# The down projection of a decoder layer: seven block products for four feature chunks instead of eight

## The chip, the core and the metric

The kernel runs on one core of a Trainium2 chip. The core has five engines with a queue each, which run in program order and wait for one another by semaphores: TensorE (PE; its weight loads are listed as PEld), VectorE (DVE), ScalarE (ACT), GpSimd (POOL) and SyncE (SP), which issues the DMAs. The metric is the time of one execution on the device in microseconds: 2034.15 us before, the median of 3 runs (2033.97 to 2034.47).

## The reference

The kernel computes one decoder layer on x of 1024 tokens x 1024 features in float32: a half-weighted feed-forward pass, a token mixer (stick-breaking attention and a gated recurrence), a second half-weighted feed-forward pass, and a final norm. Cut to what the change touches:

```python
def swiglu(h, w_gate, w_up, w_down):
    return (jax.nn.silu(h @ w_gate) * (h @ w_up)) @ w_down
...
    for l in range(DEPTH):
        h = rmsnorm(x, ffn1_norm[l])
        x = x + 0.5 * swiglu(h, ffn1_w_gate[l], ffn1_w_up[l], ffn1_w_down[l])
...
        h = rmsnorm(x, ffn2_norm[l])
        x = x + 0.5 * swiglu(h, ffn2_w_gate[l], ffn2_w_up[l], ffn2_w_down[l])
```

w_gate and w_up are 1024 x 2816, w_down is 2816 x 1024.

## The kernel before

Everything is held transposed: features on the 128 partitions, tokens along the free axis. x is 16 tiles x[c, hf] of 128 features x 512 tokens: 8 feature chunks c, 2 token halves hf. The hidden dimension of a feed-forward pass is 22 chunks of 128, and the loop over f0 takes them in pairs.

**Split numbers.** A float32 operand is split into a rounded part H (ScalarE, L121) and a rest L (VectorE, or GpSimd where `eng` says so, L122). `mm3` (L124 to L127) then does H·H, H·L and L·H, three matmuls of 128x128 by 128x512, into one PSUM bank. A weight's parts are named uH and uL (pool `unit`, 4 buffers of each), an activation's aH and aL (4 of each), those of the normalised input hH, hL, bH, bL.

**Gate and up** of a pair of chunks (`gate_up`, L391) are a 2 x 2 block product: two chunks by two halves of the 1024 input features, times these halves by two token halves. `seven` (L362) forms it with seven block products in the way of Strassen and Winograd instead of eight. `combine` (L348) makes the seven weight blocks from the two loaded tiles (raw), with four additions on GpSimd in place (L352, L353, L354, L356) and seven splits; a block product is 4 x 3 = 12 matmuls, so gate and up of a pair are 2 x 84 = 168. The blocks of the input are made once per pass. The products' sums are taken on VectorE (L373) in float32 tiles of tag c; `up` multiplies by the gate (L399) and splits the result (`finish_act`).

**Down** of a pair (`down`, L406) is plain: for each of the 8 output chunks and each token half, the two chunks are accumulated in one bank, 6 matmuls, and VectorE adds half of it to x (L415). That is 2 x 8 x 6 = 96 matmuls a pair. Its weights are split with GpSimd's help.

The first pair of a pass (f0 = 0) is computed without blocks, and the last two pairs share one down with the sums for the norm that follows. PSUM banks are handed out in a fixed turn, seven of them (`bank`). The order of instructions on each engine is not that of the code: a scheduler arranges them by a timeline of its own, and the tile pools add the waits for free buffers.

Of the kernel before, what the change touches and what calls it, by code (L numbers as in the profile page):

```python
# [8 lines left out]
F32 = mybir.dt.float32  # L9
# [4 lines left out]
ALU = mybir.AluOpType  # L14

P = 128
# [11 lines left out]
def hybrid_layer(ctx: ExitStack, tc, xT, gains, wg1, wu1, wd1, w_in, lbl, w_out, wg2, wu2, wd2, outT):  # L28
# [222 lines left out]
    def ffn(wg, wu, wd, order, prepare, on_x, on_half, pieces, g0, shared):  # L251
        one, two = order
        with ExitStack() as st:
            raws = st.enter_context(tc.tile_pool(name="raw", bufs=3))
            unit = st.enter_context(tc.tile_pool(name="unit", bufs=4))
            hx = st.enter_context(tc.tile_pool(name="hx", bufs=12))
            ap = st.enter_context(tc.tile_pool(name="ap", bufs=7))
            acc = st.enter_context(tc.tile_pool(name="acc", bufs=5, space=bass.MemoryType.PSUM))
            turns = itertools.cycle(shared)

# [10 lines left out]
            def load(src):  # L271
                r = raws.tile([P, 2 * HALF], F32, tag="raw", name="raw")
                nc.sync.dma_start(r, src)
                return r

            def entry(src, pool=None, eng=None):

                p, tH, tL = (hx, "bH", "bL") if pool is hx else (unit, "uH", "uL")
                H = p.tile([P, HALF], F32R, tag=tH, name=tH)
                L = p.tile([P, HALF], F32R, tag=tL, name=tL)  # L280
                split(H, L, src, eng)
                return H, L

            def cols4(e, k):
                return [t[:, k % 4 * P:(k % 4 + 1) * P] for t in e]

            def finish_act(a, pool=None):
                if pool is hp:
                    H, L = [hp.tile([P, HALF], F32R, tag=t, name=t) for t in ("hH", "hL")]
                else:  # L290
                    H, L = [ap.tile([P, HALF], F32R, tag=t, name=t, bufs=4) for t in ("aH", "aL")]
                split(H, L, a)
                return H, L
# [51 lines left out]
                    block("4", k, b22, nc.vector)  # L345


            def combine(r0, r1):  # L348
                a11, a12, a21, a22 = r0[:, :HALF], r0[:, HALF:], r1[:, :HALF], r1[:, HALF:]
                tt = nc.gpsimd.tensor_tensor  # L350
                e = {"11": entry(a11), "12": entry(a12), "22": entry(a22)}
                tt(a22, a21, a22, op=ALU.add)  # L352
                tt(a21, a11, a21, op=ALU.subtract)  # L353
                tt(a11, a22, a11, op=ALU.subtract)  # L354
                e["s2"] = entry(a11)
                tt(a12, a12, a11, op=ALU.subtract)  # L356
                e["s3"] = entry(a21)
                e["s1"] = entry(a22)
                e["s4"] = entry(a12)
                return e  # L360

            def seven(r0, r1, done):  # L362

                e = combine(r0, r1)

                def product(a, b):
                    ps = bank()
                    for k in range(4):
                        mm3(ps, cols4(e[a], k), B[b, k], k == 0, k == 3)
                    return ps  # L370

                def add(out, a, ps):
                    nc.vector.tensor_tensor(out, a, ps, op=ALU.add)  # L373

                u2, c11, u3, c21 = [vec() for _ in range(4)]
                nc.scalar.copy(u2, product("11", "11"))
                add(c11, u2, product("12", "21"))
                done((0, one), c11)
                p4 = product("22", "4")
                add(u2, u2, product("s2", "2"))  # L380
                add(u3, u2, product("s3", "3"))
                add(c21, u3, p4)
                done((1, one), c21)
                p5 = product("s1", "1")
                add(u3, u3, p5)
                done((1, two), u3)
                add(u2, u2, p5)
                add(u2, u2, product("s4", "22"))
                done((0, two), u2)

            def gate_up(f0, pool=None):  # L391
                S, As = {}, {}

                def gate(key, t):
                    nc.scalar.activation(t, t, AF.Silu)
                    S[key] = t

                def up(key, t):
                    nc.vector.tensor_tensor(t, S[key], t, op=ALU.mult)  # L399
                    As[f0 % 4 + key[0], key[1]] = finish_act(t, pool)  # L400

                seven(load(wg[f0]), load(wg[f0 + 1]), gate)
                seven(load(wu[f0]), load(wu[f0 + 1]), up)
                return As

            def down(Ds, As, fs, hf, chunks, on_x=None, cols=slice(0, HALF), steps=None, at=()):  # L406

# [14 lines left out]
            for f0 in range(0, NF - 2, 2):  # L422
                last = f0 + 4 >= NF
                fs = [f0 % 4, f0 % 4 + 1]
                if f0 == 0:
# [8 lines left out]
                    for hf in order:  # L434
# [16 lines left out]
                        if hf == one:  # L451
                            blocks_one()
                    blocks_two()
                else:
                    if f0 == 4 and prepare is first_h:
                        lower_bound()
                    As = gate_up(f0)
                if last:
                    As.update(gate_up(f0 + 2, hp))
                    fs = fs + [(f + 2) % 4 for f in fs]  # L460
                Ds = {}
# [591 lines left out]
```

## Time and profile before

| | |
|---|---|
| median of 3 runs | 2034.15 us |
| the profiled execution's own time | 2031.69 us |
| its span, from the first to the last instruction | 2030.0 us |
| PE busy, of the span | 1974.2 us (97%) |
| DVE, ACT, POOL busy | 1326.2, 751.7, 559.3 us |
| DMA, mean busy share of 16 engines (q1) | 16.7% |
| mean granted TensorE clock | 0.989 |

The prediction is worked out from the profiled execution, which lies 2.5 us below the median of the runs. Matmuls are pipelined: each is listed with its whole duration, and the next starts before it ends. The two feed-forward passes reach from the start to about 680 us and from about 1330 us to the end; the mixer lies between them.

### The profile page before, as it was taken

How to read it: one execution, taken by the hardware profiler on the slowest of the kernel's cores; microseconds unless marked ns; L12 is line 12 of the kernel's file. 1: busy time of each engine (PE TensorE's matmuls, PEld its weight loads, DVE VectorE, ACT ScalarE, POOL GpSimd, SP SyncE). 2: the span in 40 equal slices, each digit the busy share in tenths (PEclk: the TensorE clock that was granted, in tenths of full speed). 3: DMA queues.
4: the chain of work that ended last, by engine and by line, in shares of the span. 5: the costliest groups of instructions: out<-in, count | busy, mean ns of one | idle time of the engine just before them, and what ended most of it. 6: DMA issues, size and time to landing. Idle time of an engine off the chain costs nothing.

```text
span 2030.0 us, 28718 instructions
## 1 busy us (share of the span) xinstructions
PE 1974.2 (97%) x11226; PEld 1645.4 (81%) x11226; DVE 1326.2 (65%) x2079; ACT 751.7 (37%) x1381; POOL 559.3 (28%) x569
## 2 busy tenths in 40 slices
PE   9799999999999999999999999999999999999998
PEld 7678888888888797887987977887788888888887
DVE  7975556566557647849659479578655665665574
ACT  6333222223324335535535345443232222233243
POOL 8533222222324301202102052006232223233243
PEclk9999999999999999999999999999999999999999
DMA  4022111111212211010010121210221121221112
GB/s 167 11 62 63 53 42 52 53 52 63 62 42 90 88 52 33 12 43 22 12 52 23 32 74 42 69 37 21 63 62 44 40 63 42 62 63 54 50 52 83
DMA packets 41255, 106.73 MB, mean 53 GB/s; under 512 B 4768, under 2 KB 6816, under 8 KB 41120
## 3 DMA queue, kind: packets, MB, share of 16 engines
q1 hardware_dynamic: 40832, 104.88, 16.7%
q8 instruction: 88, 1.44, 0.3%
q14 instruction: 47, 0.39, 0.1%
q10 hardware_dynamic: 288, 0.02, 0.0%
HBM read 96.49 MB, written 8.39 MB: 52 GB/s over the span
## 4 chain that ended last, share of the span: by engine, by line
PE 85%; DVE 11%; issue 2%; POOL 1%; ACT 1%; DMA 0%; SPq 0%; POOLq 0%; DVEq 0%; ACTq 0%
PE acc L127 20%; PE acc L125 20%; PE acc L126 20%; PE pj L125 3%; PE pj L126 3%; PE pj L127 3%; PE po L690 2%; PE pv L126 2%; PE pv L125 2%; DVE rest L651 2%; PE pv L127 1%; PE wo L125 1%; PE wo L126 1%; PE wo L127 1%; DVE hL L122 1%
## 5 line engine op out<-in xcount | busy, mean ns | idle before, releaser
L121 ACT CAST uH<-raw 128x512 fp32r<-128x512 f32 x424 | 256.4, 620 | 628.8 <-PE acc L126 473.7
L122 DVE TENSOR_TENSOR uL<-raw,uH 128x512 fp32r<-128x512 f32 x352 | 254.2, 737 | 142.0 <-ACT uH L121 134.5
L373 DVE TENSOR_TENSOR c<-c,acc 128x512 f32<-128x512 f32 x280 | 188.1, 683 | 223.0 <-PE acc L127 222.0
L415 DVE SCALAR_TENSOR_TENSOR x<-acc,x 128x512 f32<-128x512 f32 (+1 forms) x328 | 216.1, 674 | 122.0 <-PE acc L127 121.8
L125 PE MATMUL acc<-hH,uH 128*128 128x512 f32 x704 | 275.0, 392 | 7.1 <-ACT hH L121 3.7
L126 PE MATMUL acc<-hL,uH 128*128 128x512 f32 x704 | 276.3, 393 | 1.4 <-DVE hL L122 1.3
L127 PE MATMUL acc<-hH,uL 128*128 128x512 f32 x704 | 265.9, 391 | 2.8 <-DVE uL L122 2.8
L126 PE MATMUL acc<-aL,uH 128*128 128x512 f32 x576 | 221.8, 389 | 0.8 <-DVE aL L122 0.8
L127 PE MATMUL acc<-aH,uL 128*128 128x512 f32 x576 | 221.6, 389 | 0.0
L352 POOL TENSOR_TENSOR raw<-raw 128x512 f32<-128x512 f32 x40 | 52.3, 1308 | 589.5 <-issue 306.8
L125 PE MATMUL acc<-aH,uH 128*128 128x512 f32 x576 | 211.6, 389 | 0.0
L127 PE MATMUL acc<-bH,uL 128*128 128x512 f32 x480 | 186.5, 389 | 0.3 <-DVE uL L122 0.3
L125 PE MATMUL acc<-bH,uH 128*128 128x512 f32 x480 | 186.7, 389 | 0.0
L126 PE MATMUL acc<-bL,uH 128*128 128x512 f32 x480 | 186.7, 389 | 0.0
L125 PEld LDWEIGHTS acc<-hH,uH 128*128 128x128 f32 x704 | 133.0, 189 | 36.4 <-ACT hH L121 4.1
L127 PEld LDWEIGHTS acc<-hH,uL 128*128 128x128 f32 x704 | 132.8, 189 | 31.7 <-DVE uL L122 4.4
L126 PEld LDWEIGHTS acc<-hL,uH 128*128 128x128 f32 x704 | 133.1, 189 | 31.0 <-DVE hL L122 2.1
L122 POOL TENSOR_TENSOR uL<-raw,uH 128x512 fp32r<-128x512 f32 x72 | 96.3, 1339 | 175.6 <-ACT uH L121 173.6
L126 PEld LDWEIGHTS acc<-aL,uH 128*128 128x128 f32 x576 | 108.1, 188 | 23.6 <-DVE aL L122 1.2
L125 PEld LDWEIGHTS acc<-aH,uH 128*128 128x128 f32 x576 | 108.1, 188 | 22.5
L127 PEld LDWEIGHTS acc<-aH,uL 128*128 128x128 f32 x576 | 108.1, 188 | 22.4
L125 PE MATMUL pj<-hH,uH 128*128 128x512 f32 x304 | 121.1, 398 | 0.5 <-DVE q L587 0.5
(228 smaller groups left out, 3981.7 us busy)
## 6 DMA issues: line engine op xcount, KB each, us to landing
raw<-in_wd_dram SPq DMA_DIRECT2D x44, 512.0 KB, 3.7
raw<-in_wg_dram SPq DMA_DIRECT2D x40, 512.0 KB, 3.6
raw<-in_wu_dram SPq DMA_DIRECT2D x40, 512.0 KB, 3.6
raw<-in_w_in_dram SPq DMA_DIRECT2D x56, 256.0 KB, 2.6
x<-in_x_dram SPq DMA_DIRECT2D x16, 256.0 KB, 5.8
xs<-x SPq DMA_DIRECT2D x16, 256.0 KB, 2.0
raw<-in_w_out_dram SPq DMA_DIRECT2D x16, 256.0 KB, 2.7
x<-xs SPq DMA_DIRECT2D x16, 256.0 KB, 3.0
```

Source lines behind the costliest of these rows:

```text
L121: nc.scalar.copy(dH, src)
L122: (eng or nc.vector).tensor_tensor(dL, src, dH.bitcast(F32), op=ALU.subtract)
L125: nc.tensor.matmul(ps, lhsT=w[0], rhs=a[0], start=first, stop=False)
L126: nc.tensor.matmul(ps, lhsT=w[0], rhs=a[1], start=False, stop=False)
L127: pe(nc.tensor.matmul(ps, lhsT=w[1], rhs=a[0], start=False, stop=last))
L352: tt(a22, a21, a22, op=ALU.add)
L373: nc.vector.tensor_tensor(out, a, ps, op=ALU.add)
L415: done = nc.vector.scalar_tensor_tensor(xt, ps, 0.5, xt, op0=ALU.mult, op1=ALU.add)
L651: nc.vector.tensor_tensor_scan(rest[:, :n], rest[:, :n], rest[:, :n], 1.0 if diag else carry, ALU.mult, ALU.bypass)
L690: nc.tensor.matmul(po[:, (qp % 2) * 256:(qp % 2) * 256 + 256], lhsT=vs[b // 2][:, b % 2, a], rhs=w[:, 256 * i:256 * i + 256], start=m == q ...
```

## The change

Chunks 2 to 17 of each pass are now taken in four groups of four; chunks 0 and 1 and the last four stay as they were. `gate_up` of a pair hands over its four results unsplit; when the second pair of a group is done, `down_seven` projects all four chunks. For each pair it treats the product as 2 x 2 blocks (two halves of the 1024 output features, two token halves, two chunks) and forms seven products of blocks, called P1 to P7 here, in the order of the code. Each is four output chunks wide, and the two pairs (n = 0, n = 1) are accumulated in the same bank: 4 x 2 x 3 = 24 matmuls.

The weight blocks come from `combine`, which is now a generator, as the products ask for them; the splits of the first pair's are on VectorE, those of the second's on GpSimd. `act_blocks` makes the blocks of activations with four subtractions per pair on GpSimd. A product's banks are read once: P1's by ScalarE into a temporary u, that GpSimd adds to x (`onto`); P2, P3, P6 and P7 are added to x by VectorE; P4 and P5 are added to u by VectorE and from there to x by GpSimd. Four raw tiles are held instead of three, twelve temporaries instead of seven; `lower_bound`, a few small instructions for the mixer, moves by one round of the loop.

```diff
-            raws = st.enter_context(tc.tile_pool(name="raw", bufs=3))
+            raws = st.enter_context(tc.tile_pool(name="raw", bufs=4))
...
-            ap = st.enter_context(tc.tile_pool(name="ap", bufs=7))
+            ap = st.enter_context(tc.tile_pool(name="ap", bufs=12))
...
-            def combine(r0, r1):
-                a11, a12, a21, a22 = r0[:, :HALF], r0[:, HALF:], r1[:, :HALF], r1[:, HALF:]
+            def combine(a11, a12, a21, a22, eng=None):
+
                 tt = nc.gpsimd.tensor_tensor
-                e = {"11": entry(a11), "12": entry(a12), "22": entry(a22)}
+                yield entry(a11, eng=eng)
+                yield entry(a12, eng=eng)
+                yield entry(a22, eng=eng)
                 tt(a22, a21, a22, op=ALU.add)
                 tt(a21, a11, a21, op=ALU.subtract)
                 tt(a11, a22, a11, op=ALU.subtract)
-                e["s2"] = entry(a11)
+                yield entry(a11, eng=eng)
                 tt(a12, a12, a11, op=ALU.subtract)
...
+            def down_seven(f0, pairs):
+
+                es = []
+                for n in range(2):
+                    r0, r1 = load(wd[f0 + 2 * n]), load(wd[f0 + 2 * n + 1])
+                    es.append(combine(r0[:, :HALF], r1[:, :HALF], r0[:, HALF:], r1[:, HALF:],
+                                      nc.gpsimd if n else nc.vector))
+
+                def act_blocks(a):
+                    def less(o, p, q):
+                        nc.gpsimd.tensor_tensor(o, p, q, op=ALU.subtract)
+
+                    b11, b12, b21, b22 = a[0, one], a[0, two], a[1, one], a[1, two]
+                    yield finish_act(b11)
+                    yield finish_act(b21)
+                    less(b11, b12, b11)
+                    t = xp.tile([P, HALF], F32, tag="x", name="a2")
+                    less(t, b22, b11)
+                    less(b21, b21, t)
+                    less(b12, b22, b12)
+                    yield finish_act(b21)
+                    yield finish_act(t)
+                    yield finish_act(b12)
+                    yield finish_act(b11)
+                    yield finish_act(b22)
+
+                blocks = [act_blocks(a) for a in pairs]
+
+                def products():
+                    ws, bs = [next(e) for e in es], [next(b) for b in blocks]
+                    for c in range(4):
+                        ps = bank()
+                        for n in range(2):
+                            mm3(ps, cols4(ws[n], c), bs[n], n == 0, n == 1)
+                        yield c, ps
+
+                def half_onto(out, ps):
+                    nc.vector.scalar_tensor_tensor(out, ps, 0.5, out, op0=ALU.mult, op1=ALU.add)
+
+                def onto(c, hf, t):
+                    nc.gpsimd.tensor_tensor(x[c, hf], x[c, hf], t, op=ALU.add)
+
+                u = {}
+                for c, ps in products():
+                    u[c] = vec()
+                    nc.scalar.mul(u[c], ps, 0.5)
+                    onto(c, one, u[c])
+                for c, ps in products():
+                    half_onto(x[c, one], ps)
+                for c, ps in products():
+                    half_onto(x[c + 4, one], ps)
+                for c, ps in products():
+                    half_onto(u[c], ps)
+                    onto(c, two, u[c])
+                for c, ps in products():
+                    half_onto(u[c], ps)
+                    onto(c + 4, one, u[c])
+                    onto(c + 4, two, u[c])
+                for c, ps in products():
+                    half_onto(x[c, two], ps)
+                    half_onto(x[c + 4, two], ps)
+                for c, ps in products():
+                    half_onto(x[c, two], ps)
...
+                elif not last:
+                    if f0 == 6 and prepare is first_h:
+                        lower_bound()
+                    if f0 % 4 == 2:
+                        As = gate_up(f0, split_up=False)
+                    else:
+                        down_seven(f0 - 2, (As, gate_up(f0, split_up=False)))
+                    continue
                 else:
-                    if f0 == 4 and prepare is first_h:
-                        lower_bound()
                     As = gate_up(f0)
-                if last:
                     As.update(gate_up(f0 + 2, hp))
```

`seven` takes its blocks from the generator, and `gate_up` has a switch `split_up`, which leaves the split out.

**GpSimd's order at the start of the down projection.** Before, at a pair's end: the four splits of down weights, and behind them the additions for the next gate.

```order
L122 TENSOR_TENSOR uL_1713<-raw_1710,uH_1712 128x512 [waits DVE_49,DMAHW6_49,PE_49,Activation_49]
L122 TENSOR_TENSOR uL_1717<-raw_1710,uH_1716 128x512 [waits DVE_49,PE_49,Activation_49]
L122 TENSOR_TENSOR uL_1723<-raw_1720,uH_1722 128x512 [waits DVE_49,DMAHW7_49,PE_49,Activation_49]
L122 TENSOR_TENSOR uL_1727<-raw_1720,uH_1726 128x512 [waits DVE_49,PE_49,Activation_49]
L352 TENSOR_TENSOR raw_1860<-raw_1860 128x512 [waits DMAHW1_49,DVE_49,Pool_49]
L353 TENSOR_TENSOR raw_1860<-raw_1858,raw_1860 128x512 [waits DMAHW0_49,Pool_49]
L354 TENSOR_TENSOR raw_1858<-raw_1860,raw_1858 128x512 [waits Pool_49]
L356 TENSOR_TENSOR raw_1858<-raw_1858 128x512 [waits Pool_49]
```

Now, in the second group of the first pass, from the split of the second pair's weight for P2 (c is a float32 temporary, a_2618 the block t of the second pair, x_0 and x_1 are x of the first and second token half):

```order
L122 TENSOR_TENSOR uL<-raw,uH 128x512 [waits DVE_49,DMAHW3_49,PE_49,Activation_49]
L418 TENSOR_TENSOR c<-c 128x512 [waits DVE_49]
L448 TENSOR_TENSOR x_0_181<-x_0_181,c 128x512 [waits Activation_49]
L448 TENSOR_TENSOR x_0_201<-x_0_201,c 128x512 [waits Activation_49]
L418 TENSOR_TENSOR a_2618<-c 128x512 [waits Pool_49]
L418 TENSOR_TENSOR c<-c 128x512
L448 TENSOR_TENSOR x_0_222<-x_0_222,c 128x512 [waits Activation_49]
L354 TENSOR_TENSOR raw<-raw 128x512 [waits DMAHW1_49,DMAHW0_49,DVE_49]
L122 TENSOR_TENSOR uL<-raw,uH 128x512 [waits PE_49,Activation_49]
L448 TENSOR_TENSOR x_0_231<-x_0_231,c 128x512 [waits Activation_49]
L418 TENSOR_TENSOR c<-c,a_2618 128x512 [waits Pool_49]
L355 TENSOR_TENSOR raw<-raw 128x512 [waits Pool_49]
```

The subtractions for the activations, the additions of P1 onto x and the weight-block additions stand in one queue; the last of the four subtractions (c<-c,a_2618), which P3 needs, is the eleventh of these rows.

**GpSimd's order at the end of the down projection**, from the split of the second pair's weight for P7 to the additions of the next gate:

```order
L122 TENSOR_TENSOR uL<-raw,uH 128x512 [waits PE_49,Activation_49]
L448 TENSOR_TENSOR x_0_264<-x_0_264,c 128x512 [waits DVE_49]
L448 TENSOR_TENSOR x_1_350<-x_1_350,c 128x512
L448 TENSOR_TENSOR x_0_273<-x_0_273,c 128x512 [waits DVE_49]
L448 TENSOR_TENSOR x_1_359<-x_1_359,c 128x512
L448 TENSOR_TENSOR x_0_282<-x_0_282,c 128x512 [waits DVE_49]
L448 TENSOR_TENSOR x_1_368<-x_1_368,c 128x512
L448 TENSOR_TENSOR x_0_291<-x_0_291,c 128x512 [waits DVE_49]
L448 TENSOR_TENSOR x_1_377<-x_1_377,c 128x512
L354 TENSOR_TENSOR raw<-raw 128x512 [waits DMAHW5_49,DVE_49]
L355 TENSOR_TENSOR raw<-raw 128x512 [waits DMAHW4_49,Pool_49]
L356 TENSOR_TENSOR raw<-raw 128x512 [waits Pool_49]
```

The eight additions of P5 onto x stand ahead of the three (L354, L355, L356) from which the gate's block s2 is made; before, no addition onto x stood on GpSimd.

**VectorE's order in the down projection.** Before, in the down stage of a pair, the reads of PSUM waited for TensorE alone:

```order
L415 SCALAR_TENSOR_TENSOR x_0_181<-acc,x_0_181 128x512 [waits PE_49]
L415 SCALAR_TENSOR_TENSOR x_0_201<-acc,x_0_201 128x512 [waits PE_49]
L415 SCALAR_TENSOR_TENSOR x_0_222<-acc,x_0_222 128x512 [waits PE_49]
L415 SCALAR_TENSOR_TENSOR x_0_231<-acc,x_0_231 128x512 [waits PE_49]
L415 SCALAR_TENSOR_TENSOR x_1_315<-acc,x_1_315 128x512 [waits PE_49]
L415 SCALAR_TENSOR_TENSOR x_1_323<-acc,x_1_323 128x512 [waits PE_49]
L415 SCALAR_TENSOR_TENSOR x_1_332<-acc,x_1_332 128x512 [waits PE_49]
L122 TENSOR_TENSOR uL<-raw,uH 128x512 [waits DMAHW6_49,PE_49,Activation_49]
L415 SCALAR_TENSOR_TENSOR x_1_341<-acc,x_1_341 128x512 [waits PE_49]
```

Now, where P6 and P7 are read (x_1_315 and the next ones are chunks 0 to 3, x_1_350 and the next ones 4 to 7):

```order
L445 SCALAR_TENSOR_TENSOR x_1_315<-acc,x_1_315 128x512 [waits DVE_49,PE_49]
L445 SCALAR_TENSOR_TENSOR x_1_323<-acc,x_1_323 128x512 [waits DVE_49,PE_49]
L445 SCALAR_TENSOR_TENSOR x_1_350<-acc,x_1_350 128x512 [waits Pool_49]
L445 SCALAR_TENSOR_TENSOR x_1_332<-acc,x_1_332 128x512 [waits DVE_49,PE_49]
L445 SCALAR_TENSOR_TENSOR x_1_359<-acc,x_1_359 128x512 [waits Pool_49]
L122 TENSOR_TENSOR uL<-raw,uH 128x512 [waits DMAHW5_49,PE_49,Activation_49]
L445 SCALAR_TENSOR_TENSOR x_1_368<-acc,x_1_368 128x512 [waits Pool_49]
L445 SCALAR_TENSOR_TENSOR x_1_341<-acc,x_1_341 128x512 [waits DVE_49,PE_49]
L445 SCALAR_TENSOR_TENSOR x_1_377<-acc,x_1_377 128x512 [waits Pool_49]
```

Every second read of a bank of P6 now waits for GpSimd's addition onto the same tile, and the split of a weight for the next gate stands between them.

## Rows read from the trace of the kernel before

**Rows 1.** Page: the span, and busy time, share and instructions of each engine.
```profile
span 2030.0 us, 28718 instructions
...
PE 1974.2 (97%) x11226; PEld 1645.4 (81%) x11226; DVE 1326.2 (65%) x2079; ACT 751.7 (37%) x1381; POOL 559.3 (28%) x569
```

**Rows 2.** Chain of waits, 130 to 260 us: start, length, engine, tile, line.
```profile
136.47 0.91 PE acc L125 x4
...
196.08 0.68 PE acc L125 x3
...
255.92 0.68 PE acc L125 x3
```

**Rows 3.** Timeline of TensorE, 92 to 106 us: three matmuls that follow each other.
```profile
start us, us, engine line op out<-in xcount [idle before <-releaser]
...
93.17 0.39 PE L126 MATMUL acc<-hL,uH 128*128 128x512 f32 x1
93.40 0.39 PE L127 MATMUL acc<-hH,uL 128*128 128x512 f32 x1
93.62 0.39 PE L125 MATMUL acc<-hH,uH 128*128 128x512 f32 x1
```

**Rows 4.** Stage table, one pair of chunks: busy time (instructions) by engine, granted clock.
```profile
core 0: us, PE busy (x) PEld busy (x) DVE busy (x) ACT busy (x) POOL busy (x), PEclk, DMA share, GB/s
...
196.10:255.90 59.80, 59.80 (x265) 49.52 (x265) 35.68 (x53) 16.59 (x29) 15.52 (x12) 1.00 0.19 53
```

**Rows 5.** Timeline of GpSimd, 195.5 to 257 us, idle time before in brackets.
```profile
215.96 1.29 POOL L352 TENSOR_TENSOR raw<-raw 128x512 f32<-128x512 f32 x1 [20.50 <-issue]
217.32 1.29 POOL L353 TENSOR_TENSOR raw<-raw 128x512 f32<-128x512 f32 x1
218.69 1.29 POOL L354 TENSOR_TENSOR raw<-raw 128x512 f32<-128x512 f32 x1
220.06 1.30 POOL L356 TENSOR_TENSOR raw<-raw 128x512 f32<-128x512 f32 x1
...
246.27 1.29 POOL L122 TENSOR_TENSOR uL<-raw,uH 128x512 fp32r<-128x512 f32 x1 [7.19 <-ACT uH L121]
```

**Rows 6.** Timeline of GpSimd, 70 to 105 us.
```profile
95.75 1.71 POOL L330 TENSOR_TENSOR b<-b,b 128x512 f32<-128x512 f32 x1
97.43 1.72 POOL L354 TENSOR_TENSOR raw<-raw 128x512 f32<-128x512 f32 x1
99.10 1.73 POOL L330 TENSOR_TENSOR b<-b,b 128x512 f32<-128x512 f32 x1
100.79 1.74 POOL L356 TENSOR_TENSOR raw<-raw 128x512 f32<-128x512 f32 x1
102.48 1.74 POOL L330 TENSOR_TENSOR b<-b,b 128x512 f32<-128x512 f32 x1
```

**Rows 7.** Timeline of VectorE, 70 to 105 us.
```profile
91.05 0.68 DVE L122 TENSOR_TENSOR uL<-raw,uH 128x512 fp32r<-128x512 f32 x1
...
98.05 0.69 DVE L415 SCALAR_TENSOR_TENSOR x<-acc,x 128x512 f32<-128x512 f32 x1
98.65 1.04 DVE L122 TENSOR_TENSOR hL<-b,hH 128x512 fp32r<-128x512 f32 x1
99.73 1.66 DVE L311 SCALAR_TENSOR_TENSOR b<-x,gn,rstd 128x512 f32<-128x512 f32 x1
101.31 1.77 DVE L122 TENSOR_TENSOR uL<-raw,uH 128x512 fp32r<-128x512 f32 x1
```

**Rows 8.** Groups by line: count, busy us, mean ns, idle before and releasers.
```profile
L121 ACT CAST uH<-raw 128x512 fp32r<-128x512 f32 x424 | 256.4, 620 | 628.8 <-PE acc L126 473.7 <-PE pj L126 48.8 <-issue 47.3
L122 DVE TENSOR_TENSOR uL<-raw,uH 128x512 fp32r<-128x512 f32 x352 | 254.2, 737 | 142.0 <-ACT uH L121 134.5 <-PE acc L125 3.2 <-PE tp L126 1.8
...
L415 DVE SCALAR_TENSOR_TENSOR x<-acc,x 128x512 f32<-128x512 f32 (+1 forms) x328 | 216.1, 674 | 122.0 <-PE acc L127 121.8
...
L122 DVE TENSOR_TENSOR aL<-c,aH 128x512 fp32r<-128x512 f32 x80 | 74.5, 932 | 16.4 <-ACT aH L121 15.1
```

**Rows 9.** TensorE after waits, 50 to 57 and 92 to 106 us, and stage table.
```profile
55.90 1.12 PE L208 MATMUL pr<-ident,rs 128*128 128x128 f32 x4 [4.96 <-DVE rs L196]
...
98.17 0.51 PE L125 MATMUL acc<-hH,uH 128*128 128x512 f32 x1 [3.70 <-ACT hH L121]
...
101.19 0.63 PE L126 MATMUL acc<-hL,uH 128*128 128x512 f32 x1
101.62 0.63 PE L125 MATMUL acc<-hH,uH 128*128 128x512 f32 x1
...
100.00:101.00 1.00, 1.00 (x3) 0.81 (x4) 1.00 (x1) 0.84 (x2) 1.00 (x2) 0.50 0.00 0
...
103.00:104.00 1.00, 0.87 (x4) 0.74 (x5) 1.00 (x3) 0.00 (x0) 1.00 (x1) 1.00 0.00 0
```

More of the change, by code (lines that the diff above doesn't have):

```diff
@@ L354, in combine @@
                 tt(a11, a22, a11, op=ALU.subtract)
-                e["s2"] = entry(a11)
+                yield entry(a11, eng=eng)
                 tt(a12, a12, a11, op=ALU.subtract)
[L357 to L360, printed above, removed]
+                yield entry(a21, eng=eng)
+                yield entry(a22, eng=eng)
+                yield entry(a12, eng=eng)
             def seven(r0, r1, done):
-                e = combine(r0, r1)
+                e = dict(zip(("11", "12", "22", "s2", "s3", "s1", "s4"),
+                             combine(r0[:, :HALF], r0[:, HALF:], r1[:, :HALF], r1[:, HALF:])))
                 def product(a, b):
@@ L389, in seven, with gate_up @@
                 done((0, two), u2)
-            def gate_up(f0, pool=None):
+            def gate_up(f0, pool=None, split_up=True):
                 S, As = {}, {}
@@ L399, in up @@
                     nc.vector.tensor_tensor(t, S[key], t, op=ALU.mult)
-                    As[f0 % 4 + key[0], key[1]] = finish_act(t, pool)
+                    As[f0 % 4 + key[0] if split_up else key[0], key[1]] = finish_act(t, pool) if split_up else t
                 seven(load(wg[f0]), load(wg[f0 + 1]), gate)
```

## The prediction

> **What bounds the kernel now.** I read the page's table of engines first: TensorE is busy for 1974.2 of 2030.0 us [rows 1], GpSimd for 28% of the span. A busy matmul is no measure of its price, because matmuls overlap, so I went to the chain of waits next. In a feed-forward pass it is TensorE alone, and one mark comes back every 59.84 us: 136.47, 196.08, 255.92 [rows 2]. That is one pair of feature chunks: 2 x 7 x 12 = 168 matmuls for gate and up, 2 x 48 = 96 for down, 264 in all, so 0.2267 us each. The timeline of TensorE says the same: matmuls last 0.39 us and start 0.23 us apart [rows 3]. Between the marks nothing holds TensorE up. In the window of one pair [rows 4] VectorE is busy for 35.68 of 59.80 us, ScalarE for 16.59 and GpSimd for 15.52. These passes are bound by the number of matmuls, as long as the other three engines keep up inside each stage and not only on average.
>
> **What is removed.** Per four chunks the down projection goes from 2 x 96 = 192 matmuls to 7 x 4 x 6 = 168. That is 24 x 0.2267 = 5.44 us. There are four such groups in each pass, eight in all: 43.5 us. Had each matmul cost its 0.39 us, it would be 75; the start distance is the right price. DMA bytes do not change.
>
> **What is added, per group.**
> - ScalarE: 14 weight casts instead of 8, 14 activation casts instead of 8, and 4 copies out of PSUM: 16 x 0.62 = 9.9 us [rows 8]. It had 33 of 120 us busy, so TensorE covers this.
> - VectorE: 28 PSUM additions instead of 32, 14 splits of activations instead of 8, 7 weight splits that GpSimd did: -4 x 0.67 + 6 x 0.93 + 7 x 0.74 = 8.1 us [rows 8]. With 71 of 120 us before, this too fits on average.
> - GpSimd: 8 additions for the weight blocks, 8 for the activation blocks, 16 onto x, one split fewer: +31. It has 55 instructions per group instead of 24. At one per 1.37 us (the start distance of 215.96, 217.32, 218.69, 220.06; a split lasts the same 1.29 as an addition [rows 5]) this is 75 us in a group of 114. On average it fits; the stage decides.
>
> **The stage.** Take t = 0 at the first matmul of a group's first down product (P1), and the end at the fourth product of the next gate, whose weight block s2 needs three GpSimd additions that stand behind the last addition onto x (the listing of GpSimd's order at the end of the down projection). TensorE's work between the two is 168 + 36 = 204 matmuls, 46.2 us. GpSimd's is 6 weight splits, 8 weight-block additions, 4 for the activations of the second pair, 16 onto x and the 3 for the gate: 37 instructions in one queue.
>
> It cannot start earlier: the first of them splits the second weight of P2, whose buffer is freed by the last product of up, at t = 0, and needs a cast (0.62) first; call it 0.8. The next wants the last activation of up, ready at about 2.
>
> Then 37 x 1.37 = 50.7 us. Already that ends at 51.5, a cast later at 52.2, so TensorE waits 6.0 us, against 5.44 saved.
>
> To this comes VectorE. When GpSimd runs without pause and VectorE has an instruction with both operands in SBUF, each holds the other up: five GpSimd instructions start 1.68, 1.67, 1.69 and 1.69 us apart [rows 6], while the splits and normalisations of VectorE beside them last 1.04 to 1.77 us instead of 0.68; an addition out of PSUM keeps its 0.69 [rows 7]. Each meeting costs GpSimd 1.69 - 1.37 = 0.32 us. In the stage there are 10 activation splits, 5 weight splits of the group and 3 of the gate, and the last product of up: 19 meetings, 6.1 us.
>
> One pause is in the queue. The split of the second weight of P6 takes over the buffer of P4's, and TensorE's order puts the matmuls that read that one behind part of P5. GpSimd comes to it after 20 instructions and 11 meetings, 0.8 + 27.4 + 3.5 = 31.7. P4's second half can start when the 17th instruction is done and cast: 0.8 + 23.3 + 8 x 0.32 + 0.7 = 27.4, and 27 matmuls later, at 33.5, the buffer is free. The pause is about 2 us.
>
> Sum: 0.8 + 50.7 + 6.1 + 2.2 + 0.7 = 60.5 us, so TensorE stands for 60.5 - 46.2 = 14.3 us. Where: without waits the second half of P4 would start at 24 x 2 + 24 + 12 = 84 matmuls = 19.0, and starts at 27.4, so 8.4 us stand ahead of P3's second half and of P4; the other 6 stand at the change from down to gate, where PSUM banks of P6 are read by VectorE only after GpSimd's additions onto x (the listings of VectorE's order), and at s2.
>
> Net per group: 14.3 - 5.44 = +8.9 us; eight groups: +71 us. From the profiled execution's own time, 2031.7 + 71 = 2102.7 us. The median of the runs shown, 2034.15, is 2.5 above that execution, so I forecast 2105 us.
>
> **Bounds.** No meeting costs anything: 52.2 us, or 54.2 with the pause; +0.6 to +2.6 us a group, 2039 to 2055. Every instruction of GpSimd meets one of VectorE: 37 x 1.69 = 62.5, in all 66.2; +14.6 a group, 2151. I take the count of meetings, because VectorE's order names them. The start of both passes has larger pools (four raw tiles, twelve temporaries); TensorE stood there 5.0 us in one place and 3.7 in another [rows 9], so I give it 5 us either way. The mixer's order does not move. One activation-table load more on ScalarE has slack all round it.
>
> **The clock.** TensorE waited 3.70 us once at 98.17, and within 2 us its granted clock was 0.50, the 1.2 GHz level; matmuls then start 0.43 us apart, and it is back at 1.00, 2.4 GHz, by 103 [rows 9]. A wait of 4 us is what I expect ahead of P3's second half in each group. While the clock is at its lower level TensorE does 24 matmuls in 10 us instead of 5.4, and the time is there, since it waits for GpSimd anyhow. The cost is then zero; if the fall came later in the stage, 3.3 us at half speed would be 1.7 us a group, 13 us in all.
> The Trainium skill (TensorE: Matmul & The Clock Gate, section HAM oscillation — how this bites in real kernels) says that a kernel whose matmuls wait in every round pays the lower clock anew in every round, which speaks against this change. By that rule the forecast would be 2118; the trace has the fall after single waits, and no run so far shows it each round.
>
> **The rivals.**
> 1. Faster: GpSimd keeps up, all of the 43.5 us shows, 1990.7. For it: GpSimd's share would be only 66% of a group. Against it: the queue's order and the 37 instructions. It decides at a stage of 46.2 + 5.44 = 51.7 us, that is a mean start distance under 1.36 us with no meeting at all, and rows 5 have 1.37 with GpSimd alone. 0.08.
> 2. The queue bounds the stage, but VectorE's meetings fall into pauses: 2039 to 2055, 0.13.
> 3. Meetings cost more: a lock that is held for a whole instruction would put VectorE's full 0.69 us on GpSimd, 19 x 0.69 = 13.1 instead of 6.1, +15.9 us a group, 2161. Against it: the pace of 1.69 [rows 6], where 1.37 + 0.69 would be 2.06. 0.07.
> The Trainium skill (SBUF — State Buffer, section Who interferes with whom) states the lock of the third: a VectorE instruction with two SBUF inputs and a GpSimd one that reads SBUF take a shared port pair for the whole instruction, and the other fully blocks. The trace agrees that only such instructions meet; it shows less than half the price.
> 4. No change: the order has 192 matmuls fewer and 248 GpSimd instructions more, so the change does what it says; only if waits and saving cancel (5.4 us a group) does the time stay. 0.04.
>
> **How the numbers follow.** My forecast has 0.68, with a range of its own from 2065 to 2140. Over the other cases I set 2043 to 2150, which leaves out the faster case, the third rival and part of the second. Faster by over 0.2% (4 us, what a measurement of this kernel can tell from no change): 0.09; within 0.2%: 0.05; slower: 0.86.
>
> **What would show it.** Marks of the chain should come 114.2 + 14 = 128 us apart for four chunks instead of 119.7. In the down stage GpSimd should be busy for nearly every microsecond over some 58 us, with starts between 1.4 and 1.7 us apart, and TensorE should wait for casts and splits that end just after a GpSimd addition (L354 to L358, L418 of the changed file). TensorE's idle time should grow by about 115 us, while its matmul count falls by 192. Wrong would be: waits under 5 us a group, GpSimd with pauses before the gate's additions, or TensorE waiting for PSUM additions of VectorE that wait for nothing on GpSimd.

## The result and the profile after

The changed kernel takes 2113.55 us (median of 3 runs, 2110.69 to 2114.98) against 2034.15: a ratio of 1.0388, 95% interval 1.0364 to 1.0411. It is 3.9% slower. The profiled execution took 2113.55 us, 81.9 more than that of before.

The page's head after, beside [rows 1], and the start of its chain of waits, as shares of the span by engine:

```profile
span 2111.8 us, 28897 instructions
...
PE 1976.2 (94%) x11034; PEld 1617.9 (77%) x11034; DVE 1471.9 (70%) x2151; ACT 818.8 (39%) x1509; POOL 941.9 (45%) x817
...
PE 62%; POOL 11%; DVE 11%; issue 3%; ACT 1%; POOLq 0%; DVEq 0%; ACTq 0%
```

TensorE has 192 matmuls less and is no less busy. GpSimd is at 45% of the span, and is still the start of the trouble. The groups of TensorE's waits (engine, line, what it waited for: us in all, times, longest):

```profile
PE acc L125 <- ACT aH L121: 24.3, 9, 3.0
PE acc L127 <- DVE uL L122: 19.9, 10, 2.9
PE acc L125 <- DVE x L445: 15.4, 12, 3.7
PE acc L125 <- ACT uH L121: 14.8, 15, 3.2
...
PE acc L125 <- DVE c L445: 10.7, 9, 1.3
```

These 85 us are waits for casts, splits and PSUM reads; before, groups of these names held 6.3 us (ACT uH 3.2, DVE uL 3.1). The stage table gives a whole group of four chunks, from the wait ahead of P3's second half to the next one; the marks of before were 2 x 59.84 = 119.7 us for the same work [rows 2, 4]. The second line is the stage of the prediction, from P1's first matmul to the product s2 of the next gate:

```profile
core 0: us, PE busy (x) PEld busy (x) DVE busy (x) ACT busy (x) POOL busy (x), PEclk, DMA share, GB/s
450.47:579.24 128.77, 120.12 (x504) 95.94 (x504) 88.96 (x113) 41.59 (x72) 78.56 (x56) 0.97 0.16 50
...
436.70:497.00 60.30, 51.66 (x206) 39.65 (x204) 44.88 (x51) 17.62 (x32) 54.12 (x38) 0.94 0.11 36
```

In the stage GpSimd is busy for 54.12 of 60.30 us; over the group only for 78.56 of 128.77. The chain of waits through the stage (start, length, engine, tile, line) shows how the time is passed on:

```profile
450.31 1.22 POOL x L448
451.53 1.23 POOL c L418
...
452.78 0.63 ACT aH L121
...
453.43 6.17 DVE aL L122 x4
459.60 1.20 DVE x L445 x2
460.80 1.72 DVE uL L122
...
462.56 1.49 PE acc L127 x4
464.05 0.43 PE acc L125
...
471.64 1.29 POOL uL L122
...
479.27 1.70 POOL uL L122
...
485.14 6.08 POOL x L448 x5
...
495.01 1.29 POOL raw L356
496.33 0.63 ACT uH L121
...
497.00 0.50 PE acc L125
```

It is read from above. GpSimd's last activation subtraction (L418) stands behind an addition onto x (L448); the cast aH and four VectorE splits follow, at 1.5 us each because GpSimd runs beside them; TensorE restarts with matmuls 0.43 us apart; only when it has freed the buffer can GpSimd split P6's weight; then its twelve additions onto x stand ahead of the gate's sums.

### The profile page after: what moved, and what is told of

It reads as the page before. It is cut to its first block, busy times and chain, and to the rows that moved or that the text cites. A ratio compares the mean times of both kernels' runs of the same rounds, so it can differ in the third digit from the quotient of the medians.

```text
span 2111.8 us, 28897 instructions
## 1 busy us (share of the span) xinstructions
PE 1976.2 (94%) x11034; PEld 1617.9 (77%) x11034; DVE 1471.9 (70%) x2151; ACT 818.8 (39%) x1509; POOL 941.9 (45%) x817
## 4 chain that ended last, share of the span: by engine, by line
PE 62%; POOL 11%; DVE 11%; issue 3%; ACT 1%; POOLq 0%; DVEq 0%; ACTq 0%
PE acc L127 13%; PE acc L125 13%; PE acc L126 13%; POOL x L448 6%; PE pj L125 3%; PE pj L126 3%; PE pj L127 3%; DVE aL L122 2%; PE po L761 2%; DVE rest L722 2%; PE pv L126 1%; PE pv L125 1%; PE pv L127 1%; POOL c L418 1%; POOL uL L122 1%
## 5 line engine op out<-in xcount | busy, mean ns | idle before, releaser
L122 DVE TENSOR_TENSOR uL<-raw,uH 128x512 fp32r<-128x512 f32 x408 | 363.6, 906 | 205.0 <-ACT uH L121 194.1
L121 ACT CAST uH<-raw 128x512 fp32r<-128x512 f32 x472 | 282.7, 619 | 482.0 <-PE acc L126 269.5
L354 POOL TENSOR_TENSOR raw<-raw 128x512 f32<-128x512 f32 x56 | 79.6, 1421 | 326.7 <-DVE uL L122 326.7
L127 PE MATMUL acc<-aH,uL 128*128 128x512 f32 x512 | 194.8, 406 | 16.8 <-DVE uL L122 16.8
L126 PE MATMUL acc<-aL,uH 128*128 128x512 f32 x512 | 207.6, 406 | 0.0
L448 POOL TENSOR_TENSOR x<-x,c 128x512 f32<-128x512 f32 x128 | 182.3, 1455 | 0.0
L125 PEld LDWEIGHTS acc<-aH,uH 128*128 128x128 f32 x512 | 100.2, 197 | 82.8 <-ACT aH L121 28.1
L121 ACT CAST aH<-c 128x512 fp32r<-128x512 f32 x112 | 68.4, 619 | 184.8 <-POOL c L418 72.9
L122 DVE TENSOR_TENSOR aL<-c,aH 128x512 fp32r<-128x512 f32 x112 | 122.5, 1099 | 23.9 <-ACT aH L121 23.9
L127 PEld LDWEIGHTS acc<-aH,uL 128*128 128x128 f32 x512 | 99.6, 196 | 41.3 <-DVE uL L122 20.2
```

The costliest lines, as they stand in the source:

```text
L121: nc.scalar.copy(dH, src)
L122: (eng or nc.vector).tensor_tensor(dL, src, dH.bitcast(F32), op=ALU.subtract)
L125: nc.tensor.matmul(ps, lhsT=w[0], rhs=a[0], start=first, stop=False)
L126: nc.tensor.matmul(ps, lhsT=w[0], rhs=a[1], start=False, stop=False)
L127: pe(nc.tensor.matmul(ps, lhsT=w[1], rhs=a[0], start=False, stop=last))
L448: nc.gpsimd.tensor_tensor(x[c, hf], x[c, hf], t, op=ALU.add)
```

## The experiments

Each kernel was timed beside the kernel before; its value then was 2032.7 to 2033.8 us. Theory: the order and length of GpSimd's queue in the down stage sets the time. Rivals: PSUM banks that VectorE frees, VectorE itself.

**GpSimd's additions and subtractions of the change left out.**
```diff
-                    onto(c, one, u[c])        # and all other onto, less,
-                tt(a22, a21, a22, op=ALU.add) # and the other sums of down weights
```


> Leaves out the additions of the weight blocks, the subtractions of the activation blocks and the sixteen additions of products into x that GpSimd does in each changed group, so the products read wrong blocks; matmuls, splits and the PSUM work of the change stay. Theory (GpSimd's order of work sets the stage): TensorE is free again and only the 24 matmuls that a group saves are left, 8 x 24 x 0.2267 us = 43.5 us under before, so about 1991 us (1985 to 2005). Rival A (the wait is for PSUM banks and VectorE's reads of them, whatever GpSimd does): it stays at 2095 us or more. Rival B (both about half): near 2050 us.

Measured: 1990.5 us, ratio 0.9786 (0.9770 to 0.9803). The saving of 24 matmuls a group is all there, 42 us, with the casts, splits and PSUM work of the change in place, and TensorE idles about as long as before:

```profile
PE 1931.7 (97%) x11034; PEld 1609.0 (81%) x11034; DVE 1381.9 (69%) x2151; ACT 817.9 (41%) x1509; POOL 558.7 (28%) x561
```

So the GpSimd work costs 2113.6 - 1990.5 = 123 us, 15.4 a group.

**Four GpSimd instructions more.**
```diff
+                    if c < 2:
+                        nc.gpsimd.tensor_tensor(x[c, two], x[c, two], u[c], op=ALU.subtract)
+                        onto(c, two, u[c])
```


> Four more GpSimd instructions a group, behind the additions of the fourth product (two blocks of x have a product taken off and put on again). Theory (GpSimd's chain ends last in the stage): each costs its whole pace, 8 x 4 x 1.45 = 46 us, so about 2160 us (2145 to 2170). Rival (GpSimd has slack and TensorE waits for something else): 2113 to 2118 us.

Measured: 2167.52 us, 54 more than the changed kernel, 1.69 us for each of the 32. There is no slack. The 1.69 is not the length of one addition, though: GpSimd's busy time grew from 941.9 to 980.7 us, 1.21 for each. The rest is a pause in its queue that grew with them, the one before the split of P6's weight. The groups by line of the changed kernel and of this one (busy us, mean ns | idle before):

```profile
L122 POOL TENSOR_TENSOR uL<-raw,uH 128x512 fp32r<-128x512 f32 x64 | 98.0, 1539 | 100.7 <-ACT uH L121 62.3
```
```profile
L122 POOL TENSOR_TENSOR uL<-raw,uH 128x512 fp32r<-128x512 f32 x64 | 94.1, 1476 | 118.6 <-ACT uH L121 62.4
```

The idle time before these splits is 17.9 us longer. The waits in it for ScalarE's casts are as before; those for TensorE's matmuls grew from 38.2 to 56.0 us.

**All additions onto x on VectorE.**
```diff
-                    nc.gpsimd.tensor_tensor(x[c, hf], x[c, hf], t, op=ALU.add)
+                    nc.vector.tensor_tensor(x[c, hf], x[c, hf], t, op=ALU.add)
```


> All sixteen additions of products into x of a group go from GpSimd to VectorE. Theory: GpSimd is left with 55 - 16 = 39 instructions a group, some 39 x 1.45 = 57 us of a mark that would be 114 us, so its chain no longer ends last; VectorE gets 16 x 0.74 = 11.8 us more. Expected 2010 us (1995 to 2050), under before. Rival A (the wait is for PSUM banks that VectorE frees): VectorE is later still, so 2115 us or more. Rival B (VectorE becomes the bound in the down stage): between 2050 and 2100 us.

Measured: 2093.64 us, ratio 1.0298 (1.0282 to 1.0313). The expectation missed; rival B holds. In the groups by line the additions take 0.88 us (count | busy us, mean ns | idle before), and TensorE waits at the change to the gate for PSUM reads that stand behind them:

```profile
L448 DVE TENSOR_TENSOR x<-x,c 128x512 f32<-128x512 f32 x128 | 109.0, 879 | 3.5 <-ACT c L453 3.1
```
```profile
PE acc L125 <- DVE x L445: 36.4, 8, 4.7
```

**Half of them on VectorE.**
```diff
-                    onto(c, one, u[c])                # P1
+                    half_onto(x[c, one], ps)
-                    onto(c + 4, one, u[c])            # P5
+                    onto(c + 4, one, u[c], nc.vector)
```


> Eight of the sixteen additions into x go to VectorE: the four of the first product (added straight from PSUM) and four of the fifth. Theory: 8 x 1.45 = 11.6 us less of GpSimd a group, of a stall that is 8 to 14 us a group: 2113 - 8 x (8 to 11) = 2025 to 2050 us, say 2040. Rival A (PSUM banks): 2113 us or more. If the additions moved are not those that the next casts wait behind, a smaller gain, 2075 to 2100 us.

Measured: 2073.6 us, ratio 1.0201 (1.0186 to 1.0216), 40 us under the changed kernel. The expectation missed: this is about half of the 73 us that it had in the middle. TensorE now waits in more places for VectorE's PSUM reads (25.8 us in 25 places for c L445, against 10.7 in 9).

**Fewer meetings.**
```diff
-                    yield finish_act(b11)
+                    yield rough(b11)    # ScalarE: H = copy(a), L = a * 2**-12; all 7 blocks
```


> The low parts of the activation blocks are written by ScalarE as a scaled copy of the block (not the true rest), so fourteen VectorE operations with two SBUF operands leave each changed group and ScalarE gets fourteen more copies; GpSimd's work is the same. Theory (a GpSimd addition beside such a VectorE operation takes 1.7 us instead of 1.3 us, and so stretches the stage): some 10 meetings a group less, 8 x 10 x 0.35 = 28 us, so about 2085 us (2070 to 2095). Rival A (the meetings cost the stage nothing): 2110 to 2116 us. Rival B (one engine holds the port for its whole instruction): 8 x 14 x 0.7 = 78 us or more, 2035 us.

Measured: 2073.74 us, 40 under the changed kernel, 5.0 us a group: in the range, more than the 28 expected and half of rival B's 78. Two GpSimd additions that start 1.70 us apart in the changed kernel now start 1.22 us apart. First the changed kernel's timeline of GpSimd, then this one's, one group later:

```profile
455.62 1.73 POOL L356 TENSOR_TENSOR raw<-raw 128x512 f32<-128x512 f32 x1
457.32 1.74 POOL L355 TENSOR_TENSOR raw<-raw 128x512 f32<-128x512 f32 x1
```
```profile
568.75 1.28 POOL L356 TENSOR_TENSOR raw<-raw 128x512 f32<-128x512 f32 x1
569.97 1.29 POOL L355 TENSOR_TENSOR raw<-raw 128x512 f32<-128x512 f32 x1
```

A part of the 40 us is VectorE's own: its splits were on the chain too. The run does not separate the two.

**The buffers alone.**
```diff
-            raws = st.enter_context(tc.tile_pool(name="raw", bufs=3))   # before
+            raws = st.enter_context(tc.tile_pool(name="raw", bufs=4))   # and ap 7 -> 12
```


> The kernel before with only the buffers of the change: four of raw weights instead of three, twelve of scratch instead of seven. Theory (buffers matter neither way, TensorE waits for nothing there): 2030 to 2038 us, as before. Rival (the larger buffers move work on the side engines against each other): over 1% either way.

Measured: 2036.1 us, ratio 1.0017 (1.0007 to 1.0026): 3 us. The buffers are not what costs the change its time.

**The fifth product's additions written later.**
```diff
                     half_onto(u[c], ps)
-                    onto(c + 4, one, u[c])    # and two; now written
-                    onto(c + 4, two, u[c])    # behind the seventh product
```


> The changed kernel with the eight GpSimd additions of the fifth product written behind the seventh product: the same instructions, and GpSimd's order hardly moves, but VectorE's reads of the sixth and seventh products from PSUM no longer wait behind those additions. Theory (some 6 us of a group's stall are PSUM banks held so): 8 x 4 to 6 us less, 2065 to 2085 us. Rival (the stall at the change to the gate is the weights' casts, later than the banks): 2105 to 2113 us.

Measured: 2122.87 us (2118.39 to 2127.5), ratio 1.0444 (1.0420 to 1.0468). This theory fell. The waits for PSUM reads at the change to the gate left (15.4 us in the changed kernel), and TensorE waits in their place for the casts of the gate's weights, which stand behind the same additions in GpSimd's queue (14.8 us in the changed kernel):

```profile
PE acc L125 <- ACT uH L121: 32.6, 17, 3.2
```

So 15.4 us went and 17.8 came. Why the median is even 9 us slower stays open.

**Reordered.** As the run above, and:
```diff
-                    yield finish_act(b11)
-                    yield finish_act(b21)
+                    first, second = finish_act(b11), finish_act(b21)
                     less(b11, b12, b11)       # and the other three
+                    yield first
+                    yield second
...
-                    onto(c, one, u[c])        # P1
+                    half_onto(x[c, one], ps)
```


> Three edits to the changed kernel: the additions of the fifth product behind the seventh as in the run beside it, the subtractions of the activation blocks written ahead of the first product, and the first product added to x by VectorE straight from PSUM (four GpSimd instructions a group fewer, four VectorE operations of 0.68 us more). Theory (what counts is what GpSimd has to end before the next cast or PSUM read can start, not its sum): the 3 us ahead of the third product and most of the rest go, 2020 to 2055 us. Rival A (GpSimd's sum of work in the stage counts whatever its order): only 8 x 4 x 1.5 = 48 us, 2065 us. Rival B (VectorE takes its place as the bound): 2070 to 2100 us.

Measured: 2063.53 us, ratio 1.0150 (1.0135 to 1.0166). The expectation missed, and by this number alone rival A had it, GpSimd's sum. The chain shows another thing: eight additions, behind them the gate's sums, a cast, and TensorE restarting at half clock, with matmuls 0.43 us apart.

```profile
579.40 6.83 POOL x L449 x6
...
587.88 1.90 POOL x L449 x2
...
590.83 1.30 POOL raw L354
...
593.56 1.27 POOL raw L356
594.85 0.63 ACT uH L121
595.53 0.80 PE acc L125
596.32 0.43 PE acc L126
```

**The gate's sums first.** As the run above, and the eight additions tied behind the last sum of the next gate:
```diff
+                    v = vec()                 # P5 into a buffer of its own
+                    nc.vector.scalar_tensor_tensor(v, ps, 0.5, u[c], op0=ALU.mult, op1=ALU.add)
...
                 seven(load(wg[f0]), load(wg[f0 + 1]), gate)
+                while pending:
+                    with tc.issue_after(last_sum[0]):    # GpSimd's a12 - a11
+                        pending.pop()()                  # the eight onto of P5
```


> The reordered kernel of before this run, with the eight additions of the fifth product tied behind GpSimd's four weight-block additions of the next gate (and its sum in a buffer of its own, so that VectorE needn't wait for the fourth product's additions). GpSimd does as much work as there. Theory (what GpSimd has to end before the next cast decides, not its sum of work): the gaps of 2.65 and 1.18 us and the half-clock stretch behind the first go, 8 x 3.5 to 5 us under 2063.5 us: 2023 to 2036 us. Rival (GpSimd's sum of work in the stage decides): the wait comes back elsewhere, 2055 us or more.

Measured: 2030.3 us, ratio 0.9992 (0.9983 to 1.0002): 33 us less, with as much work on GpSimd. Rival A of the run before is out. Not all of the 33 us need be the order: TensorE's waits for VectorE's reads of PSUM into u, 11.0 us in the run before (c L446), are gone too, and such waits are what the buffer of its own was to remove. The two edits were not run apart. GpSimd's timeline, idle time and its releaser in brackets: the additions now stand behind the sums (L356 to L360), and GpSimd waits for VectorE's split of a block that the first sum overwrites.

```profile
458.24 1.29 POOL L356 TENSOR_TENSOR raw<-raw 128x512 f32<-128x512 f32 x1 [8.41 <-DVE uL L122]
459.61 1.30 POOL L357 TENSOR_TENSOR raw<-raw 128x512 f32<-128x512 f32 x1
460.99 1.27 POOL L358 TENSOR_TENSOR raw<-raw 128x512 f32<-128x512 f32 x1
462.34 1.28 POOL L360 TENSOR_TENSOR raw<-raw 128x512 f32<-128x512 f32 x1
463.57 13.20 POOL L456 TENSOR_TENSOR x<-x,c 128x512 f32<-128x512 f32 x8
```

**The sums early.** As the run above, and the sums of each chunk pair in another order:
```diff
+                tt(a21, a21, a22, op=ALU.add)          # first sum, before any cast
                 yield entry(a11, eng=eng)
                 yield entry(a12, eng=eng)
                 yield entry(a22, eng=eng)
-                tt(a22, a21, a22, op=ALU.add)
-                tt(a21, a11, a21, op=ALU.subtract)
-                tt(a11, a22, a11, op=ALU.subtract)
+                tt(a11, a21, a11, op=ALU.subtract)     # second
+                tt(a22, a22, a11, op=ALU.subtract)     # third
```


> As the run beside it, with the four sums of a weight chunk pair formed in another order (the third as the block 22 less the second sum), so that the first sum waits for no cast and the second for the cast of block 11 alone. As many GpSimd instructions. Theory: the waits ahead of the third product (0.65 and 1.15 us a group, with gaps under 0.5 us beside them) go too, 8 x 1.5 to 3 us under the run beside it, 2000 to 2022 us, faster than the kernel before. Rival A (those gaps are set by VectorE's splits): the same as the run beside it. Rival B (the earlier sums meet more of VectorE's splits in the up stage and delay them): slower than it.

Measured: 2064.33 us, ratio 1.0156 (1.0141 to 1.0171). Missed, for a reason that neither rival had: the third sum (L358) is now formed late, and the tie was to the fourth (L360), so the third went behind the eight additions, and a cast that TensorE wants went with it. GpSimd's timeline, then ScalarE's, then TensorE's wait:

```profile
585.24 1.29 POOL L360 TENSOR_TENSOR raw<-raw 128x512 f32<-128x512 f32 x1
586.50 10.87 POOL L456 TENSOR_TENSOR x<-x,c 128x512 f32<-128x512 f32 x8
597.33 1.25 POOL L358 TENSOR_TENSOR raw<-raw 128x512 f32<-128x512 f32 x1
```
```profile
598.62 2.18 ACT L121 CAST uH<-raw 128x512 fp32r<-128x512 f32 x4 [7.70 <-POOL raw L358]
```
```profile
PE acc L125 <- ACT uH L121: 36.7, 9, 5.1
```

**Both sums ahead.** As the run above, but:
```diff
-                    with tc.issue_after(last_sum[0]):
+                    with tc.issue_after(last_sum[0]), tc.issue_after(last_sum[1]):
```


> As the run with the early sums, but the eight additions of the fifth product are tied behind both of the gate's last two weight-block sums: there the sum for the gate's fifth product stood behind the eight additions, and TensorE waited 4.3 us a group for its cast and ran on at half clock. As much GpSimd work. Theory (what stands ahead of the next cast in GpSimd's order decides): 4.3 us and about 2 us of the half clock go in each of the eight groups, 2064 - 8 x (5 to 6.5) = 2012 to 2024 us, under the kernel before. Rival (the sum of GpSimd's work in the stage decides): the wait comes back elsewhere, 2045 us or more.

Measured: 2003.61 us (2003.14 to 2009.53), ratio 0.9860 (0.9843 to 0.9876), faster than the kernel before by 1.4%. One sum a group, moved past eight additions, is worth 61 us (the instructions that changed place with it are one other sum, two casts and a split a group). That is more than the 40 to 52 us expected. TensorE's waits in the group of that cast fell from 36.7 to 1.0 us, and its busy time, with as many matmuls, from 1958.6 to 1932.9 us. So 36 us were waits and 26 us matmuls further apart: in the run before, the granted clock is 0.50 behind each of the eight waits. A group now takes 115.31 us at full clock, with GpSimd nearly as busy as in the changed kernel (52 instructions and 75.56 us a group; 56 and 78.56 there):

```profile
421.03:536.34 115.31, 114.53 (x504) 94.52 (x504) 93.22 (x117) 41.89 (x72) 75.56 (x52) 1.00 0.19 55
```

**The order of the sums in the kernel before.**
```diff
+                tt(a21, a21, a22, op=ALU.add)
                 e = {"11": entry(a11), "12": entry(a12), "22": entry(a22)}
-                tt(a22, a21, a22, op=ALU.add)
-                tt(a21, a11, a21, op=ALU.subtract)
-                tt(a11, a22, a11, op=ALU.subtract)
+                tt(a11, a21, a11, op=ALU.subtract)
+                tt(a22, a22, a11, op=ALU.subtract)
```


> The kernel before with only the other order of the four weight-block sums, eight products as ever. Theory (the 2003.6 us of the run with the sums early and both ties come from the seven products, once GpSimd no longer holds TensorE up): before waits little for these sums, so 2025 to 2036 us. Rival (the order of the sums itself gives the gain, whatever the products): near 2005 us.

Measured: 2028.49 us, ratio 0.9984 (0.9975 to 0.9994): 4 us. The other 26 of the 30 us by which the run above is under before come with the seven products.

## Why the prediction was right, point by point

- **The saving.** 43.5 us predicted, 42 measured with the GpSimd work left out; matmuls priced at their start distance [rows 3] hold.
- **The stage.** 60.5 us predicted, 60.30 measured; the group 128 and 128.77. Six distances between the marks of after are 134.30, 130.30 and 128.77 in the first pass, 128.89, 130.25 and 128.75 in the second. Their excess over 119.7 is 10.5 us on average, 84 us for eight groups, against 71 predicted; the two executions differ by 81.9. The steady group was met; what was missed is that others take 1.5 and, once, 5.5 us more.
- **The queue's length.** Between the first of the 37 instructions (437.42) and the end of the 37th (496.29) lie 58.9 us; predicted 59.0. That the two agree so closely is luck, since two terms were off against each other by some 3 us each. Work: 53.7 us instead of 50.7 + 6.1, because additions that meet nothing start 1.22 to 1.25 us apart there, not 1.37 [rows 5]; the 1.37 returns in the gate's own sums. Pauses: 0.63 + 4.52 us instead of 2.2 (where the working itself, 33.5 - 31.7, gives 1.8).
- **The meetings.** 6.1 us a group predicted for 19 of them; 14 of VectorE's operations taken away gave 5.0, with what these operations cost VectorE itself. Who pays was wrong in part: the prediction put the price on GpSimd's queue alone, and the chain has four VectorE splits on it that take 6.17 us, where four at 0.68 would take 2.7.
- **The place.** TensorE waits ahead of P3's second half and of P4 (2.98 and 1.57 us in the group shown) and at the change to the gate (1.34 and 0.72), as named, and at P5 (1.18), which was not named. The sizes are smaller than predicted: in the stage TensorE is idle for 60.30 - 51.66 = 8.6 us, not 14.3, and the rest is matmuls that start further apart. For the change to the gate, the late fifth product shows that the gate's sums bind there, and that banks freed earlier gain nothing.
- **The clock.** This step failed: I took its cost as zero, since TensorE waits for GpSimd anyhow. The stage table has the lower level in each group of both passes; three of the rows:

```profile
324.00:326.00 2.00, 2.00 (x6) 1.60 (x5) 2.00 (x3) 0.66 (x2) 2.00 (x2) 0.50 0.00 0
464.00:466.00 2.00, 2.00 (x7) 1.54 (x6) 2.00 (x3) 0.71 (x2) 2.00 (x2) 0.50 0.00 0
...
1816.00:1818.00 2.00, 2.00 (x6) 1.60 (x5) 2.00 (x2) 0.93 (x2) 2.00 (x2) 0.50 0.00 0
```

  From 462.56 on, eleven matmuls of the chain take 4.4 us instead of 2.5, and GpSimd's split of P6's weight waits for the buffer that they read. GpSimd's timeline, then the same place of the chain one group earlier, where four matmuls take 2.08 us instead of 0.91:

```profile
471.64 1.29 POOL L122 TENSOR_TENSOR uL<-raw,uH 128x512 fp32r<-128x512 f32 x1 [4.52 <-PE acc L127]
```
```profile
333.96 2.08 PE acc L127 x4
```

  The chain covers seven groups. In four of them the granted clock is 0.50 at this restart or just behind it, and the matmuls there cost the chain 1.7 to 1.9 us; in three it is 1.00, and they cost 0.3. That is 8 us in all, less than the 13 that the prediction had as its upper case. The groups that start at 450.47 and 1812.47 have the lower level at the restart, those at 579.24 and 1941.21, with nearly the same waits before, have not: from the start to the freed buffer the first two take 21.0 us, the others 19.4. No run took the clock away alone, so its cost is read from this trace and not shown by experiment. The Trainium skill (TensorE: Matmul & The Clock Gate, section HAM oscillation — how this bites in real kernels) has the lower clock paid anew in every round; the trace agrees, with the lower level in all eight groups. The 2118 worked out beside that rule was 4 us off, my 2105 was 9.
- **TensorE's idle time.** Predicted +115 us, measured (2111.8 - 1976.2) - (2030.0 - 1974.2) = +79.8. The prediction put all of TensorE's lost time down as idle. The span grew by 81.8 us though 43.5 us of matmuls are gone, 125 us in all; the 45 us that are not idle time are matmuls that are counted as busy and start further apart, many of them 0.43 us, at half clock.
- **The rivals.** GpSimd keeps up: no, 32 instructions more cost 54 us. VectorE's meetings fall into pauses: no, taking 14 operations a group away gave 40 us. A lock for the whole instruction: not by its time, 2161; of its pace more in the last section. No change: no, 3.9%.

## What to carry to other kernels

A side engine at 45% of the span can cost 123 us: count its queue in the stage where its results are wanted, not over the period. Then ask of each cast which instructions stand ahead of its input in that queue: with as much work, one sum a group moved ahead of eight additions was worth 61 us, and eight additions moved behind four sums, with a buffer of their own for what they add, 33 us. A saving of matmuls showed up here only once no cast waited behind work that nobody was waiting for.

## What the hardware showed that I had not expected

A GpSimd addition beside a VectorE operation with two SBUF operands starts 1.70 us after the one ahead, and 1.22 to 1.25 us where it meets none; a VectorE split beside it lasts 1.72 us (at 460.80 in the chain) and not 0.68. VectorE's operations that meet nothing start 0.60 apart, as in its timeline with all additions onto x on VectorE:

```profile
550.31 0.69 DVE L122 TENSOR_TENSOR aL<-c,aH 128x512 fp32r<-128x512 f32 x1
550.91 0.69 DVE L401 TENSOR_TENSOR c<-c 128x512 f32<-128x512 f32 x1
```

One after the other, the two would take 1.25 + 0.60 = 1.85 us: 1.70 is almost that. The Trainium skill (SBUF — State Buffer, section Who interferes with whom) says that the one of the two that comes second blocks fully. With 1.25 as the base these rows are far nearer to it than in the prediction, which set 1.69 against 1.37 + 0.69 = 2.06: its 1.37 came from additions that follow each other in one block's sums. Still, 1.70 lies under 1.85, so the full price is not shown.
